# Fetching the tiles of v as pairs from one queue, in a decoder trunk with expert retrieval

## The chip, the cores and the metric

One core of one Trainium2 chip runs the whole program. The metric is device time in microseconds (us), the median of several executions. A profile of one execution shows where the time goes.

## What is computed

Two decoder layers over 256 positions of width 1024. Layer 0 mixes with attention and retention, layer 1 with a short gated convolution. Behind each mixer stands a product-key expert retrieval ("peer"): every token has 8 heads, each picks 16 of 16384 experts, and the output is the gated sum of their rows of v.

```python
def peer(xn, w_q, sub_keys, u, v):
    ...
    s1, i1 = lax.top_k(sc[:, :, 0], PEER_TOPK)
    s2, i2 = lax.top_k(sc[:, :, 1], PEER_TOPK)
    ...
    gate = jax.nn.softmax(top_s, axis=-1).astype(xn.dtype)
    ...
        hid = jax.nn.gelu(jnp.einsum('td,thkd->thk', tc, u[ec]), approximate=False)
        return jnp.einsum('thk,thkd->td', gc * hid, v[ec])
```

`u` and `v` are 16384 x 1024 in float32 for each layer, 64 MiB each.

## The kernel before

A layer's retrieval is done in two ways at once. For 160 tokens (`TD`) it is dense: all 128 tiles of u (128 experts x 1024, 512 KB) are multiplied with the tokens, the gates are put in where an expert was picked, and all 128 tiles of v are multiplied with the result. For the other 96 tokens (`TG`) rows of u and v are gathered: `Gather` issues indirect DMAs from POOL, each of 128 rows of 4 KB, 192 a layer, and DVE multiplies what has landed (line 1041 adds a row of v times its weight to `gacc`). `ga.step()` is called once a tile with a rate that spreads the rest of the gather over the tiles that are left; six tiles (`rows`, `grow`) hold rows.

The dense part has two stretches, here called u and v. In the v stretch tile i is used by PE for eight blocks of the output. Most tiles (those in `SPL`) are split first: ACT copies the raw tile into `vhi` in a shorter format (`weight_parts`, line 1419), DVE subtracts it from the raw tile into `vlo` (`weight_rest`, line 1426), and PE multiplies both (lines 1546 and 1548). A raw tile isn't read again after that subtraction. The tiles 0, 2, 12, 22, ... 122 and the last three are not split, PE reads them raw (line 1506). `carry(i)` does ACT's copy of tile i + 3 and DVE's subtraction of tile i + 2; then comes `st.next()` for tile i, then its matmuls. `vhi` and `vlo` have three buffers each.

All weights come through one ring, `Stream.ring`, with eight slots of 512 KB (`RAW`). `srcs` lists what is fetched and in which order. An entry of double width is fetched by one DMA into two neighbouring slots, as 8 KB a partition: the tiles of u are such pairs. The tiles of v are single, 4 KB a partition, and those with an odd number are issued by ACT (`src[2]`), all others by SP. `room()` says whether the next fetch may be written into the program: `free(i)` holds for a whole tile (its second entry is None) once `nu`, the count of tiles handed out, is past it. Engines run their own programs in order, and a DMA on a queue waits there for the last readers of its slot; so the place of a fetch in the program matters on ACT, among its copies, and little on SP, which does nothing else in these loops.

Of the kernel before, what the change touches and what calls it, by code (L numbers as in the profile page):

```python
# [19 lines left out]
P = 128  # L20
S = 256
D = 1024
# [6 lines left out]
NK = 128  # L29
# [8 lines left out]
STEPS = TG  # L38
SUB = 32
RAW = 8  # L40
# [9 lines left out]
for i in SPL:  # L50
    a, n = list(RUNS.items())[-1] if RUNS else (-9, 0)
# [69 lines left out]
class Stream:  # L121
# [6 lines left out]
    def __init__(self, ctx, tc, srcs):  # L128
        self.nc = tc.nc
        self.srcs = srcs  # L130
        pool = ctx.enter_context(tc.tile_pool(name="wraw", bufs=1))
        self.ring = pool.tile([P, RAW, D], F32, tag="raw", name="raw")
        self.hi_pool = ctx.enter_context(tc.tile_pool(name="whi", bufs=3))
        self.lo_pool = ctx.enter_context(tc.tile_pool(name="wlo", bufs=3))
        self.more = None
        self.end = 0
        self.raw = {}
        self.part = {}
        self.nl = 0
        self.held = 0  # L140
        self.ns = 0
        self.nu = 0

# [11 lines left out]
    def room(self):  # L155

        if self.nl >= len(self.srcs):
            return False
        n = 2 if self.srcs[self.nl][0].shape[-1] > D else 1
        return self.free(self.nl + n - 1 - RAW)  # L160

    def whole(self, i):
        return self.srcs[i][1] is None
# [23 lines left out]

    def free(self, i):

        return i < 0 or (i < self.nu - self.held if self.whole(i) else i < self.ns)  # L190

    def ahead(self, extra=0):
        n = len(self.srcs)
# [27 lines left out]


@with_exitstack
def trunk_kernel(ctx, tc, x, small, cst, mcst, ew_in, ew_out, ow_in, ow_out, wq, keys, pu, pe_, pv, pun, gains, out):
    nc = tc.nc
    v = nc.vector
    act = nc.scalar
# [15 lines left out]
    def peer_srcs(l):  # L243
        r = [(wq[l, f], f not in (1, 2)) for f in range(NPAIR)]
        for i in range(len(REST) // 2):
            r += [(pu[l, i], None), (None, None)]
        r += [(pv[l, i], None, i % 2 == 1) for i in range(NK)]
        return r

    srcs += peer_srcs(0)  # L250
    OF = [b * ND + k for k in range(ND) for b in (1, 2, 0)]
    srcs += [(ow_in[f], i > 1 and i % 2 == 1) for i, f in enumerate(OF)]
    srcs += [(ow_out[c], c % 2 == 0 and c < 6) for c in range(ND)]
    srcs += peer_srcs(1)

    h = pers.tile([P, 2, D], F32, tag="h", name="h")
# [10 lines left out]
    st = Stream(ctx, tc, srcs)  # L267
# [12 lines left out]
    def nm(s):  # L280
        uid[0] += 1
        return f"{s}{uid[0]}"
# [700 lines left out]
    class Gather:  # L983
# [29 lines left out]
        def issue(self):  # L1013

            while (self.open and self.i < self.TOTAL and (self.i < self.known or self.known == STEPS)
                   and self.i < self.c + len(self.rows)):
                s_ = self.i
                self.i += 1
                table = pun if s_ < STEPS else pv.rearrange("l i p d -> (l i p) d")
                gp.indirect_dma_start(self.row(s_), None, table,  # L1020
                                      bass.IndirectOffsetOnAxis(IG[:, 0, s_ % STEPS:s_ % STEPS + 1].bitcast(U32), 0))

# [30 lines left out]
    def peer(l, before, norm):  # L1053
        with tc.tile_pool(name=nm("hg"), bufs=1) as hp:
# [360 lines left out]
            def weight_parts(j, low=True):  # L1415

                raw = st.raw[first + j]
                whi[j] = st.hi_pool.tile([P, D], F32R, tag="hi", name=nm("vhi"))
                act.copy(whi[j], raw)  # L1419
                if low:  # L1420
                    weight_rest(j)

            def weight_rest(j):
                raw = st.raw[first + j]
                wlo[j] = st.lo_pool.tile([P, D], BF16, tag="lo", name=nm("vlo"))
                v.tensor_tensor(wlo[j], raw, whi[j].bitcast(F32), OP.subtract)  # L1426

            first = st.nu + NK - len(PRE)
            for i in range(NK):
# [82 lines left out]
            def carry(i):  # L1512
                j = i + AHEAD
                if "rest" in hsb:
                    row_rest()
                if 4 <= j and j in SPL:
                    if j in RUNS:
                        row_parts(j)
                    weight_parts(j, False)
                if 4 <= j - 1 and j - 1 in SPL:  # L1520
                    weight_rest(j - 1)
# [61 lines left out]
    with tc.manual_schedule():  # L1583
        norms = [Norm(0)]
        nc.sync.dma_start(G, small)
        nc.sync.dma_start(C[:, :P], cst[:, :P])
        for th in range(2):
            (nc.scalar if th else nc.sync).dma_start(h[:, th, :], x[th])
        nc.sync.dma_start(C[:, P:], cst[:, P:])
        v.memset(Z, 0.0)  # L1590
        act.activation(norms[0].w[:, 0, 6:7], Z[:, 0:1], AF.Sqrt)
        for _ in range(3):
            st._load()
        busy(24)
        norms[0].first(hid_tile(nm("junk")))
        a = Norm(1)
        even_mixer(norms[0], a)
        b = Folded(2)
        peer(0, a, b)
        a = Norm(3)  # L1600
        odd_mixer(b, a)
        peer(1, a, Final())
# [40 lines left out]
```

## Time and profile before

| What | Value |
|---|---|
| median of 3 runs | 1489.08 us (1485.73 to 1489.53) |
| the profiled execution, its own time | 1486.53 us |
| its span in the trace | 1484.7 us, granted clock 0.996 |
| busy share of PE, PEld, DVE, ACT, POOL | 97%, 89%, 84%, 54%, 49% |
| moved by DMA | 531.81 MB, mean 358 GB/s |
| fetches of v | 128 from SP, 128 from ACT, 512 KB each |
| fetches of u | 104 pairs from SP, 1024 KB each |
| indirect DMAs of rows | 192 of u, 192 of v |

PE is TensorE's matmuls, PEld its loading of weights, DVE VectorE, ACT ScalarE, POOL GpSimd, SP SyncE; a name with q is the queue of an engine. In a row "a<-b" the first name is written and the second read; "raw<-pv" is a fetch of a tile of v into the ring, "rows<-pv,ig" a gather of rows. The DMA share is the mean busy time of 16 DMA engines; since packets overlap a little at their ends, a full engine shows slightly over 1. The chain is the work that ended last, followed back from the end of the program.

### The profile page before, as it was taken

The page shows a single profiled execution, that of the slowest core. Times are in us where ns is not written, and L with a number is a line of the kernel's source. Part 1 is how long each engine was busy: PE and PEld are TensorE (multiplying, and loading weights), DVE is VectorE, ACT ScalarE, POOL GpSimd, SP SyncE. Part 2 cuts the span into 40 slices and gives each one's busy share as a digit, 9 for nine tenths or more (in the row PEclk, how much of TensorE's full clock was granted, in tenths as well). Part 3 has the DMA queues.
Part 4 walks back from the last instruction along what each step waited for, and adds up shares of the span by engine and source line. Part 5 has one row for each costly group of instructions (what it writes and reads, how often), then busy time and mean ns, then how long its engine had stood idle before and what let it go on. Part 6 is the DMA issues. An engine that isn't in the chain of part 4 may idle for free.

```text
span 1484.7 us, 30109 instructions
## 1 busy us (share of the span) xinstructions
PE 1434.1 (97%) x11260; PEld 1327.8 (89%) x11260; DVE 1242.5 (84%) x2505; ACT 804.1 (54%) x1872; POOL 731.1 (49%) x508
## 2 busy tenths in 40 slices
PE   9999999999998999899999999999999999999997
PEld 5667999999998999898898699999999999988887
DVE  5637999968898789999976589997888868999997
ACT  6556412158775555555663463213887745655554
POOL 6754545546664344443244374555655624653540
PEclk9999999999999999999999999999999999999999
DMA  8547899999999999999975589999999999999994
GB/s 323 198 146 253 324 369 393 397 413 412 411 412 407 385 398 405 402 407 408 384 264 180 179 307 346 388 402 404 411 413 410 402 392 396 389 407 406 405 408 172
DMA packets 132164, 531.81 MB, mean 358 GB/s; under 512 B 15217, under 2 KB 15473, under 8 KB 118705
## 3 DMA queue, kind: packets, MB, share of 16 engines
q1 hardware_dynamic: 57024, 257.95, 45.0%
q0 software_dynamic: 56416, 204.29, 34.8%
q10 hardware_dynamic: 18576, 67.64, 11.6%
q8 instruction: 89, 1.46, 0.4%
q14 instruction: 59, 0.48, 0.1%
HBM read 527.93 MB, written 1.05 MB: 356 GB/s over the span
## 4 chain that ended last, share of the span: by engine, by line
DMA 37%; PE 29%; DVE 24%; issue 5%; ACT 2%; POOL 1%; ACTq 0%; SPq 0%; DVEq 0%; POOLq 0%
DMA raw<-pv 25%; DMA rows<-pun,ig 7%; PE hid L1408 7%; DVE rows L1030 4%; PE vo L1546 4%; DMA grow<-pv,ig 3%; PE hid L291 2%; PE vo L1506 2%; DVE hg L1140 2%; DVE grow L1030 2%; DVE hg L1146 2%; DVE hg L1142 2%; PE vo L1548 2%; PE ea L325 2%; DMA rows<-pv,ig 2%
## 5 line engine op out<-in xcount | busy, mean ns | idle before, releaser
L1408 PE MATMUL hid<-xf,raw 128*128 128x160 f32 x3328 | 478.2, 301 | 8.8 <-DVE hg L1449 8.5
L1408 PEld LDWEIGHTS hid<-xf,raw 128*128 128x128 f32 x3328 | 458.2, 191 | 11.7 <-DVE hg L1449 11.6
L1419 ACT CAST vhi<-raw 128x1024 fp32r<-128x1024 f32 x222 | 227.4, 1047 | 205.7 <-DMA raw<-pv 143.1
L1546 PE MATMUL vo<-ko,vhi 128*128 128x320 f32 x1776 | 315.2, 319 | 14.8 <-DVE ko L1496 9.6
L1426 DVE TENSOR_TENSOR vlo<-raw,vhi 128x1024 bf16<-128x1024 f32 x222 | 268.0, 1223 | 47.6 <-ACT vhi L1419 43.2
L1020 POOL DMA_INDIRECT rows<-pv,ig x128 | 199.8, 1561 | 216.4 <-DVE gacc L1041 172.0
L1546 PEld LDWEIGHTS vo<-ko,vhi 128*128 128x128 f32 x1776 | 262.0, 188 | 21.3 <-ACT vhi L1419 14.2
L1020 POOL DMA_INDIRECT rows<-pun,ig x128 | 161.3, 1260 | 118.6 <-DVE rows L1030 61.6
L176 POOL TENSOR_TENSOR lo<-raw,hi 128x1024 bf16<-128x1024 f32 x70 | 167.2, 2397 | 87.0 <-ACT hi L174 80.3
L1030 DVE SCALAR_TENSOR_TENSOR rows<-rows,xg 128x1024 f32<-128x1024 f32 x128 | 155.4, 1220 | 23.6 <-DMA rows<-pun,ig 23.1
L1548 PE MATMUL vo<-hb,vlo 128*128 128x160 bf16 x1776 | 161.4, 234 | 7.1 <-DVE vlo L1426 6.8
L1446 ACT ACTIVATE hg<-hid 128x160 f32<-128x160 f32 (+14 forms) x240 | 62.2, 265 | 194.1 <-PE hid L1408 193.9
L1041 DVE SCALAR_TENSOR_TENSOR gacc<-rows,ghid,gacc 128x1024 f32<-128x1024 f32 x124 | 158.8, 1281 | 6.5 <-DMA rows<-pv,ig 6.2
L1020 POOL DMA_INDIRECT grow<-pv,ig x64 | 91.8, 1434 | 117.9 <-DVE gacc L1041 103.1
L1548 PEld LDWEIGHTS <-vlo 128*128 128x128 bf16 x1776 | 117.4, 98 | 34.1 <-DVE vlo L1426 14.3
L1358 ACT ACTIVATE ko<-ko,idxT 128x128 f16<-128x128 f16 x320 | 101.6, 391 | 38.2 <-DVE ko L1343 38.1
L1020 POOL DMA_INDIRECT grow<-pun,ig x64 | 82.8, 1293 | 78.9 <-DVE grow L1030 50.2
L174 ACT CAST hi<-raw 128x1024 fp32r<-128x1024 f32 x100 | 102.4, 1046 | 30.2 <-issue 19.9
L291 PE MATMUL hid<-x,hi 128*128 128x256 f32 x800 | 108.9, 289 | 3.9 <-DVE z L973 2.0
L291 PEld LDWEIGHTS hid<-x,hi 128*128 128x128 f32 x800 | 100.0, 193 | 4.8 <-issue 2.9
L1361 ACT ACTIVATE ko<-ko,idxT 128x128 f16<-128x128 f16 x320 | 101.2, 389 | 0.0
L1506 PE MATMUL vo<-hg,raw 128*128 128x160 f32 x544 | 83.1, 302 | 1.1 <-DVE hg L1449 1.1
(254 smaller groups left out, 2075.6 us busy)
## 6 DMA issues: line engine op xcount, KB each, us to landing
raw<-pu SPq DMA_DIRECT2D x104, 1024.0 KB, 8.3
raw<-pv SPq DMA_DIRECT2D x128, 512.0 KB, 8.5
raw<-pv ACTq DMA_DIRECT2D x128, 512.0 KB, 7.9
raw<-wq SPq DMA_DIRECT2D x32, 512.0 KB, 4.2
raw<-ew_in SPq DMA_DIRECT2D x28, 512.0 KB, 4.4
raw<-ow_in SPq DMA_DIRECT2D x24, 512.0 KB, 4.9
hg<-pe_ SPq DMA_DIRECT2D x22, 512.0 KB, 6.9
raw<-ew_out SPq DMA_DIRECT2D x8, 512.0 KB, 3.3
```

The source lines that it names most:

```text
L174: self.nc.scalar.copy(hi, t)
L176: eng.tensor_tensor(lo, t, hi.bitcast(F32), OP.subtract)
L291: pe.matmul(ps[:, :S], hi[:, k * P:(k + 1) * P], A2[:, k, s_, :], start=k == 0 and s_ == 0, stop=False)
L1020: gp.indirect_dma_start(self.row(s_), None, table, bass.IndirectOffsetOnAxis(IG[:, 0, s_ % STEPS:s_ % STEPS + 1].bitcast(U32), 0))
L1030: v.scalar_tensor_tensor(r, r, 1.0, XG[:, q % 2, :], op0=OP.mult, op1=OP.mult, accum_out=w)
L1041: v.scalar_tensor_tensor(self.acc[q], r, w, self.acc[q], op0=OP.mult, op1=OP.add)
L1408: pe.matmul(ps[:, :TD], w[k], XF[:, k, :], start=k == 0, stop=k == ND - 1)
L1419: act.copy(whi[j], raw)
L1426: v.tensor_tensor(wlo[j], raw, whi[j].bitcast(F32), OP.subtract)
L1506: pe.matmul(vo[b][:, TG:S], w[:, c], HG[:, i, :], stop=i == NK - 1, **m)
L1546: pe.matmul(vo[b][:, TG:S + TD], hi[:, b * P:(b + 1) * P], hs, **m)
L1548: pe.matmul(vo[b][:, TG:S], lo[:, b * P:(b + 1) * P], hb, **m)
```

## The change

The tiles of v are listed as pairs like those of u, so that one DMA from SP brings two tiles. ACT issues none. A pair needs both slots free. `dead` is a set of ring entries whose raw tile has been told to be split to the end: `weight_rest` puts a tile in and at once lets the stream write the fetches that this makes possible. Since the array of v is laid out for pairs now, the gather reads from a second copy of v in plain order, `pvn`.

```diff
+        self.dead = set()
...
         n = 2 if self.srcs[self.nl][0].shape[-1] > D else 1
-        return self.free(self.nl + n - 1 - RAW)
+        return all(self.free(self.nl + j - RAW) for j in range(n))
...
-        return i < 0 or (i < self.nu - self.held if self.whole(i) else i < self.ns)
+        return i < 0 or i in self.dead or (i < self.nu - self.held if self.whole(i) else i < self.ns)
...
-        r += [(pv[l, i], None, i % 2 == 1) for i in range(NK)]
+        for i in range(NK // 2):
+            r += [(pv[l, i], None), (None, None)]
...
-                table = pun if s_ < STEPS else pv.rearrange("l i p d -> (l i p) d")
+                table = pun if s_ < STEPS else pvn
...
                 v.tensor_tensor(wlo[j], raw, whi[j].bitcast(F32), OP.subtract)
+                st.dead.add(first + j)
+                st.loads()
...
-        "pv": ct(a["peer_v"].reshape(2, NK, P, D)),
+        "pv": ct(a["peer_v"].reshape(2, NK // 2, 2, P, D).transpose(0, 1, 3, 2, 4)).reshape(2, -1, P, 2 * D),
+        "pvn": ct(a["peer_v"].reshape(2 * NK * P, D)),
```

The order of instructions on PE and DVE stays as it was. On ACT, in the v stretch of layer 0, the rows around the copy of tile 23 were these (`vhi_5219`; the fetch behind it is that of tile 27, and the one behind `vhi_5266` that of tile 29):

```order
L1488 CAST ko_4767<-hg_1210 128x3x160
L1489 CAST hb_5216<-hg_1210 128x480 [waits PE_49]
L1419 CAST vhi_5219<-raw 128x1024 [waits DMAHW3_49,DVE_49,PE_49]
L151 DMA raw<-pv 128x1024
L1419 CAST vhi_5243<-raw 128x1024 [waits DMAHW1_49,DVE_49,PE_49]
L1419 CAST vhi_5266<-raw 128x1024 [waits DMAHW5_49,DVE_49,PE_49]
L151 DMA raw<-pv 128x1024 [waits DMAHW7_49]
```

And now (`vhi_5207` is the copy of tile 23):

```order
L1492 CAST ko_4763<-hg_1210 128x3x160
L1493 CAST hb_5204<-hg_1210 128x480 [waits PE_49]
L1421 CAST vhi_5207<-raw 128x1024 [waits DMAHW5_49,DVE_49,PE_49]
L1421 CAST vhi_5230<-raw 128x1024 [waits DMAHW6_49,DVE_49,PE_49]
L1421 CAST vhi_5252<-raw 128x1024 [waits DVE_49,PE_49]
```

The fetches are gone from ACT, and its copies follow each other.

On SP, before, the rows are the fetches of the tiles 12, 14, 16, 18, 20 and 22. The one of tile 20 waits for PE, since its slot held tile 12, which isn't split:

```order
L151 DMA raw<-pv 128x1024 [waits DMAHW6_49,DMAHW5_49,DVE_49]
L151 DMA raw<-pv 128x1024 [waits DMAHW0_49,DVE_49]
L151 DMA raw<-pv 128x1024 [waits DMAHW2_49,DVE_49]
L151 DMA raw<-pv 128x1024 [waits DMAHW4_49,DMAHW3_49,DVE_49]
L151 DMA raw<-pv 128x1024 [waits DMAHW5_49,PE_49]
L151 DMA raw<-pv 128x1024 [waits DMAHW7_49,DMAHW6_49,DVE_49]
```

And now, the pairs from (12, 13) to (22, 23):

```order
L152 DMA raw<-pv 128x2048 [waits DMAHW4_49,DVE_49]
L152 DMA raw<-pv 128x2048 [waits DMAHW5_49,DVE_49]
L152 DMA raw<-pv 128x2048 [waits DMAHW6_49,DVE_49]
L152 DMA raw<-pv 128x2048 [waits DMAHW7_49,DVE_49]
L152 DMA raw<-pv 128x2048 [waits DMAHW0_49,DVE_49,PE_49]
L152 DMA raw<-pv 128x2048 [waits DMAHW1_49,DVE_49]
```

There are as many rows as before, each twice as wide. The pair (20, 21) waits for DVE and for PE, and what stands behind it waits with it.

More of the change, by code (lines that the diff above doesn't have):

```diff
@@ L223, in trunk_kernel @@
 @with_exitstack
-def trunk_kernel(ctx, tc, x, small, cst, mcst, ew_in, ew_out, ow_in, ow_out, wq, keys, pu, pe_, pv, pun, gains, out):
+def trunk_kernel(ctx, tc, x, small, cst, mcst, ew_in, ew_out, ow_in, ow_out, wq, keys, pu, pe_, pv, pvn, pun, gains, out):
     nc = tc.nc
```

## The prediction

> **What bounds the kernel now.** I read the page first (busy shares, slices, chain), then the windows, then the DMA queues of two windows, then the chain in order of time.
>
> ```profile
> span 1484.7 us, 30109 instructions
> PE 1434.1 (97%) x11260; PEld 1327.8 (89%) x11260; DVE 1242.5 (84%) x2505; ACT 804.1 (54%) x1872; POOL 731.1 (49%) x508
> ...
> DMA  8547899999999999999975589999999999999994
> ...
> DMA raw<-pv 25%; DMA rows<-pun,ig 7%; PE hid L1408 7%; DVE rows L1030 4%; PE vo L1546 4%; DMA grow<-pv,ig 3%; PE hid L291 2%; PE vo L1506 2%; DVE hg L1140 2%; DVE grow L1030 2%; DVE hg L1146 2%; DVE hg L1142 2%; PE vo L1548 2%; PE ea L325 2%; DMA rows<-pv,ig 2%
> ...
> raw<-pu SPq DMA_DIRECT2D x104, 1024.0 KB, 8.3
> raw<-pv SPq DMA_DIRECT2D x128, 512.0 KB, 8.5
> raw<-pv ACTq DMA_DIRECT2D x128, 512.0 KB, 7.9
> ```
>
> PE's 97% is modelled and hides waits, so it decides nothing. The chain puts 25% of the span, 371 us, on fetches of tiles of v: 256 fetches of 512 KB (134.2 MB), half from SP, half from ACT. That is exactly what the change touches. The windows say whether those waits are latency or bandwidth (columns: busy time of PE, PEld, DVE, ACT, POOL, then clock, DMA share, GB/s):
>
> ```profile
> 335.00:370.00 35.00, 35.00 (x298) 34.66 (x298) 29.64 (x67) 29.88 (x114) 22.03 (x18) 1.00 1.02 413
> 482.00:510.00 28.00, 27.08 (x219) 26.02 (x219) 18.89 (x23) 15.53 (x25) 6.35 (x4) 1.00 0.99 384
> 510.00:546.00 36.00, 36.00 (x319) 34.57 (x319) 31.79 (x31) 20.12 (x25) 18.06 (x11) 1.00 1.01 398
> 580.00:620.00 40.00, 36.84 (x306) 33.24 (x307) 36.25 (x34) 22.78 (x30) 14.68 (x10) 1.00 1.02 407
> 660.00:700.00 40.00, 37.28 (x317) 34.22 (x314) 36.51 (x35) 23.99 (x30) 14.88 (x11) 1.00 1.02 408
> 1300.00:1340.00 40.00, 36.74 (x303) 32.65 (x302) 36.59 (x35) 24.00 (x30) 21.69 (x11) 1.00 1.02 404
> ```
>
> In the v stretch the DMA engines are full (1.02) and move 404 to 408 GB/s; in the u stretch, with the same share, 413. So v is bound by what a byte costs on the DMA engines, except at its start, where PE sets the pace. The chain (start, length, what) gives the bounds of the stretch, 482 to about 738 us in layer 0 and 1204 to about 1455 in layer 1, and its two kinds of links:
>
> ```profile
> 482.37 8.75 DMA raw<-pv
> ...
> 508.92 1.21 PE vo L1546 x8
> 510.13 0.57 PE vo L1548 x8
> ...
> 565.52 7.79 DMA raw<-pv
> ...
> 573.41 0.02 ACT vhi L1419
> 573.43 9.09 DMA raw<-pv
> ...
> 732.65 1.28 DVE gacc L1041
> 737.62 2.21 PE vo L1506 x16
> ...
> 1203.91 8.05 DMA raw<-pv
> ...
> 1455.24 1.29 DVE gacc L1041
> ```
>
> First PE works tile behind tile, 1.78 us each. Later each link is one landing of about 8 us, a cast that starts on it, and at once the next fetch from ACT. At some 2.0 us a tile a link spans 4 tiles: a fetch from ACT goes out when the tile 4 ahead of its own has landed.
>
> **What a byte costs.** Queue q1 is SP's, q10 ACT's, q0 the rows of the gather (columns: packets, MB, share of 16 engines). First 300 to 460 us (u, fetched as pairs), then 580 to 700 us (v, single tiles):
>
> ```profile
> DMA packets 14197, 66.01 MB, mean 413 GB/s; under 512 B 1563, under 2 KB 1563, under 8 KB 10738
> q0 software_dynamic: 10322, 37.59, 58.7%
> q1 hardware_dynamic: 3857, 28.19, 42.8%
> ```
>
> ```profile
> DMA packets 13341, 48.69 MB, mean 406 GB/s; under 512 B 1481, under 2 KB 1481, under 8 KB 13329
> q0 software_dynamic: 4827, 17.58, 36.7%
> q1 hardware_dynamic: 4314, 15.71, 33.0%
> q10 hardware_dynamic: 4188, 15.24, 32.1%
> ```
>
> Share times window times 16 over MB gives engine time per MB. Pairs of u (8 KB a partition): 0.428 x 160 x 16 / 28.19 = 38.9 us. Single tiles of v (4 KB): 0.330 x 120 x 16 / 15.71 = 40.3 from SP, 0.321 x 1920 / 15.24 = 40.4 from ACT. The gather, 4 KB rows in both, is the control: 0.587 x 2560 / 37.59 = 40.0 and 0.367 x 1920 / 17.58 = 40.1. So it isn't the stretch that makes v dearer, it is the short rows: 1.5 us per MB, 3.8%.
>
> **The change part by part.**
>
> Single tiles become pairs. If every byte of v were on the path: 134.2 MB x 1.5 / 16 = 12.6 us less. On the path are 371 us of the 507 us of both v stretches, 73%: 9.2 us. By the rates alone (406 to 413 GB/s, 1.7% of 371 us) it is 6.3 us. I take 9, the queues' own figure, since the control supports it, and keep 6.3 and 12.6 as ends.
>
> The start of v. Here PE is the bound and cheaper bytes bring nothing by themselves; they can only fill the ring further before the engines become the bound. One more tile in the ring is worth its fetch, 0.524 MB at 406 GB/s, 1.3 us, once a layer; none is worth 0, two in each layer 5 us. There is room for it: the DMA share falls to 0.99 there, and the gather pauses (waits from 470 to 500 us: total, times, longest):
>
> ```profile
> POOL rows L1020 <- DVE gacc L1041: 13.9, 1, 13.9
> ```
>
> I take 1 us for both layers together. Steady work minus 9, start minus 1: minus 10.
>
> ACT issues 128 fetches less, SP as many as before but of double size (durations in ns of the issues, then waits, from 580 to 720 us).
>
> ```profile
> L151 ACTq DMA_DIRECT2D raw<-pv x34: 333/334/335, 582.6 to 717.6; - x34
> ACT vhi L1419 <- DMA raw<-pv: 48.7, 28, 2.6
> SPq L151 <- DVE vlo L1426: 91.8, 25, 6.4
> SPq L151 <- PE vo L1506: 35.5, 7, 7.0
> ```
>
> 128 x 0.334 us = 43 us of ACT's queue is taken away and I cost it at 0: it runs beside the cast that precedes it (573.41 and 573.43 above), and ACT waits 48.7 of the 140 us from 580 for landings anyway. Were that cover gone, it would be a gain, of 43 us at most.
>
> When a pair may start. Tile k+8 from SP waits for the subtraction of tile k; tile k+4 from ACT for the landing of tile k. Afterwards the pair waits for the subtractions of both tiles it replaces, and everything behind it on SP with it. The first tile of a pair so goes out about one tile later than it did, 2 us; the second, which went out 4 tiles ahead of use, now goes out some 6 ahead. Bounds: each start 2 us late and uncovered at the 24 unsplit tiles from 12 to 122 would cost 48 us; the looser second tile could gain up to what DVE leaves (below). Between them I take 0, because the row it is nearest to is the DMA share of 1.02: work is always queued on the engines, so a later start lengthens a queue and costs no time. If that cover is gone, the third rival decides.
>
> The set of dead slots moves fetches earlier in the program only. In the v loop SP issues nothing but these fetches, and each still waits for its slot's readers: 0. Nothing else stands behind them on SP there.
>
> The table of rows has the same 4 KB rows, bytes and issues on POOL: 0. POOL is idle half of the span (49% busy above), and no queue is moved past it.
>
> Sum: the profiled execution took 1486.53 us, 1.8 us around its span, so 1476.5. The median of the runs is 1489.08, 2.6 above the profiled one, which gives 1479.
>
> **What is late next.** DVE, not PE (546 to 721 us):
>
> ```profile
> 546.00:721.00 175.00, 163.87 (x154) 1.00 1.02 405
> L1426 DVE TENSOR_TENSOR vlo<-raw,vhi 128x1024 bf16<-128x1024 f32 x78 | 93.9, 1223 | 11.0 <-ACT vhi L1419 8.6 <-PE vo L1506 1.5 <-PE vo L1546 0.5
> ```
>
> It is busy 163.87 of 175 us, 93.6%; a stretch shorter by 2.5% leaves it at 96%. No gain beyond 6.4% of 371 us, 24 us, is possible there.
>
> **The rivals.**
>
> Nothing to see. The rows' length doesn't matter, and the 406 of v is the mix. For it: when nothing but single 4 KB tiles is fetched (750 to 800 us, 40 slices), slices reach 413 too.
>
> ```profile
> GB/s 0 56 354 410 367 413 397 410 397 161 305 102 144 347 320 385 387 413 397 318 197 82 347 177 295 269 138 0 184 292 285 236 243 33 285 161 341 52 0 0
> ```
>
> Against it: the gather's own rows cost the same in u and v. Then only the start of v gains, 1 us: 1488, with 1485 to 1492 around it. A rule speaks for this rival: the Trainium skill, "DMA: Bandwidth & Descriptors", Specifications, puts the smallest transfer for line rate at 512 B, by which rows of 4 KB are as good as 8 KB and the steady term would be 0 instead of 9 us. The queue rows above, 40.4 against 38.9, disagree with it.
>
> The ring was the bound. The links of 4 tiles set the pace, and the full engines are only what that leaves; then issuing further ahead frees v up to DVE's limit. Against it: a share of 1.02 with nothing to spare. At most 24 us: 1465.
>
> Pairs starve the engines. Every tenth tile (12, 22, ...) isn't split, its slot is free only when PE has done with it (the 7 waits of 35.5 us above), and now its neighbour and all later pairs wait with it; the tile before a pair's second can't be used until both have landed. For it: SP already waits 5.1 us each time. Against it: three pairs and several rows are queued meanwhile. Price: d us at each of the 24 unsplit tiles; it decides from 0.4 us on, where 24 d eats the 10 us. At 1 us, half a tile's time: 1479 + 24 = 1503.
>
> **How the numbers follow.** About 0.3%, 4.5 us, is what a measurement of this kernel tells from no change: below 1484.6 is faster, above 1493.5 slower. Cheaper bytes, 1472 to 1484: 0.52. The ring, 1463 to 1472: 0.12. Nothing to see, 1485 to 1492: 0.21. Starved engines, 1494 and up: 0.15. Faster 0.64, same 0.21, slower 0.15. The likeliest is 1479. The range from 1465 to 1491 holds the first, nearly all of the second and most of the third.
>
> **What would show it.** Right: in the v stretch the fetches cost about 39 us per MB on q1, the rate is 412 to 415 GB/s at a share of 1.02, the chain's share on fetches of v falls by some 9 us, DVE is busier than 95%, and u and the mixers keep their lengths. The ring as the bound: a v stretch more than 8 us shorter in each layer with the cost per MB unchanged. Nothing to see: q1 at 40 and 406 GB/s. Starved: the DMA share below 1.0 in steady v, and casts that wait longer after each unsplit tile. The prediction fails above all if the engines run dry between pairs, or if DVE and PE, each above 90%, cannot close up as far as the DMA allows.

## The result and the profile after

The changed kernel took 1478.76 us in the median of 7 runs (1473.74 to 1481.83), the kernel before 1486.33 beside it: ratio 0.9931, interval 0.9912 to 0.9949, faster by some 10 us (8 to 13 by the interval). The forecast was 1479, from a median before of 1489.08 (a ratio of 0.9932). The profiled execution took 1473.74 us, span 1472.0; it is the fastest of the seven, so its span is 12.7 us below the one before, where the means of the runs differ by 9.3.

The page, the lines that answer to those of before:

```profile
span 1472.0 us, 29967 instructions
PE 1428.2 (97%) x11260; PEld 1327.3 (90%) x11260; DVE 1238.5 (84%) x2505; ACT 805.0 (55%) x1872; POOL 775.8 (53%) x508
...
PE 48%; DVE 26%; DMA 18%; issue 5%; ACT 2%; POOL 1%; DVEq 0%; SPq 0%; POOLq 0%; ACTq 0%
PE hid L1410 14%; PE vo L1550 10%; DMA rows<-pvn,ig 7%; DMA grow<-pvn,ig 6%; PE vo L1552 5%; DVE rows L1032 3%; PE vo L1510 3%; DMA rows<-pun,ig 2%; PE hid L293 2%; DVE gacc L1043 2%; DVE vlo L1428 2%; DVE hg L1142 2%; DVE grow L1032 2%; DVE hg L1148 2%; DVE hg L1144 2%
...
raw<-pv SPq DMA_DIRECT2D x128, 1024.0 KB, 9.3
```

Fetches of v held 25% of the chain; now they aren't in this list. PE's products of v (`vo`) and gathered rows of v (`rows<-pvn`, `grow<-pvn`, 13% together) stand there. Where the time came from shows in PE's order of time: the first products of a split tile of v in layer 0, the first of layer 1's mixer, the first products of a split tile of v in layer 1, before and after:

```profile
494.05 1.44 PE L1546 MATMUL vo<-ko,vhi 128*128 128x320 f32 x8
751.43 2.18 PE L308 MATMUL hid<-x,hi 128*128 128x256 f32 x16
1214.90 1.44 PE L1546 MATMUL vo<-ko,vhi 128*128 128x320 f32 x8
```

```profile
493.93 1.45 PE L1550 MATMUL vo<-ko,vhi 128*128 128x320 f32 x8
745.02 2.18 PE L310 MATMUL hid<-x,hi 128*128 128x256 f32 x16
1206.64 1.44 PE L1550 MATMUL vo<-ko,vhi 128*128 128x320 f32 x8
```

v of layer 0 took 257.4 us and takes 251.1; from there to v of layer 1 463.5 and 461.6; from there to the end of the span 269.8 and 265.4. So 10.7 of the 12.7 us of span come out of the two v stretches (the last one with the end of the program behind it). In the windows and queues of the changed kernel (columns as before the change; queues from 580 to 700 us):

```profile
482.00:510.00 28.00, 27.25 (x221) 26.19 (x220) 18.91 (x23) 15.62 (x25) 6.47 (x4) 1.00 1.02 410
510.00:546.00 36.00, 36.00 (x319) 34.57 (x317) 31.69 (x31) 20.12 (x25) 18.82 (x11) 1.00 0.99 391
580.00:620.00 40.00, 39.81 (x350) 37.47 (x349) 39.97 (x40) 25.00 (x32) 22.91 (x12) 1.00 1.02 415
660.00:700.00 40.00, 38.11 (x327) 35.28 (x326) 38.94 (x37) 24.36 (x31) 26.97 (x12) 1.00 1.02 415
```

```profile
DMA packets 9207, 49.77 MB, mean 415 GB/s; under 512 B 1017, under 2 KB 1017, under 8 KB 5262
q1 hardware_dynamic: 4418, 32.21, 65.1%
q0 software_dynamic: 4776, 17.39, 36.1%
...
raw<-pv SPq DMA_DIRECT2D x30, 1024.0 KB, 9.7
rows<-pvn,ig POOLq DMA_INDIRECT x24, 18.2
grow<-pvn,ig POOLq DMA_INDIRECT x11, 19.4
```

0.651 x 1920 / 32.21 is 38.8 engine us per MB for the fetches, where 40.4 stood; the gather stays at 0.361 x 1920 / 17.39 = 39.9. The engines are as full as before and move 415 GB/s, not 406. PE (39.81 of 40 us) and DVE (39.97) still set the pace at 580 to 620 us, where the kernel before already waited for fetches. The new thing is in the last two rows: gathered rows land after 18 to 19 us, where they took 11. The chain from 600 us on goes over them:

```profile
605.20 1.36 PE vo L1550 x8
...
617.45 19.90 DMA grow<-pvn,ig
...
671.94 17.94 DMA rows<-pvn,ig
689.98 1.30 DVE gacc L1043
691.53 20.16 DMA rows<-pvn,ig
```

DVE's waits from 470 to 735 us say the same. First the kernel before, then the changed one (total us, times, longest):

```profile
DVE vlo L1426 <- ACT vhi L1419: 21.0, 25, 3.3
```

```profile
DVE vlo L1428 <- ACT vhi L1421: 12.0, 8, 3.2
DVE gacc L1043 <- DMA rows<-pvn,ig: 6.4, 5, 2.2
DVE gacc L1043 <- DMA grow<-pvn,ig: 1.4, 2, 1.2
```

### The profile page after: what moved, and what is told of

Same layout as the page of the kernel before. It is cut to its first block, busy times and chain, and to the rows that moved or that the text cites. A ratio compares the mean times of both kernels' runs of the same rounds, so it can differ in the third digit from the quotient of the medians.

```text
span 1472.0 us, 29967 instructions
## 1 busy us (share of the span) xinstructions
PE 1428.2 (97%) x11260; PEld 1327.3 (90%) x11260; DVE 1238.5 (84%) x2505; ACT 805.0 (55%) x1872; POOL 775.8 (53%) x508
## 4 chain that ended last, share of the span: by engine, by line
PE 48%; DVE 26%; DMA 18%; issue 5%; ACT 2%; POOL 1%; DVEq 0%; SPq 0%; POOLq 0%; ACTq 0%
PE hid L1410 14%; PE vo L1550 10%; DMA rows<-pvn,ig 7%; DMA grow<-pvn,ig 6%; PE vo L1552 5%; DVE rows L1032 3%; PE vo L1510 3%; DMA rows<-pun,ig 2%; PE hid L293 2%; DVE gacc L1043 2%; DVE vlo L1428 2%; DVE hg L1142 2%; DVE grow L1032 2%; DVE hg L1148 2%; DVE hg L1144 2%
## 5 line engine op out<-in xcount | busy, mean ns | idle before, releaser
L1022 POOL DMA_INDIRECT rows<-pvn,ig x128 | 226.1, 1767 | 185.3 <-DVE gacc L1043 144.1
L1022 POOL DMA_INDIRECT grow<-pvn,ig x64 | 111.6, 1743 | 95.0 <-DVE gacc L1043 76.1
L1043 DVE SCALAR_TENSOR_TENSOR gacc<-grow,ghid,gacc 128x1024 f32<-128x1024 f32 x62 | 79.3, 1279 | 9.3 <-DMA grow<-pvn,ig 9.1
```

What stands on the lines that cost most here:

```text
L1022: gp.indirect_dma_start(self.row(s_), None, table, bass.IndirectOffsetOnAxis(IG[:, 0, s_ % STEPS:s_ % STEPS + 1].bitcast(U32), 0))
L1043: v.scalar_tensor_tensor(self.acc[q], r, w, self.acc[q], op0=OP.mult, op1=OP.add)
```

## Taking the change apart

The total came out as forecast, but a total can be right by terms that cancel. The theory is that rows of 8 KB are cheaper than rows of 4 KB. The rivals are that fetches go out further ahead, that there are fewer DMAs, that the dead slots or the second table matter. Four kernels ran on one chip to hold these apart, beside the kernel before; the changed kernel itself did not run there.

**Single tiles, all from SP.**

```diff
-        for i in range(NK // 2):
-            r += [(pv[l, i], None), (None, None)]
+        r += [(pv[l, i], None) for i in range(NK)]
```

> The changed kernel, but the tiles of v are fetched singly again (512 KB, 4 KB a partition), all of them by SP, with the dead slots and the second table kept. Theory 'short rows cost more': the queue of SP costs 40.0 to 40.6 engine us per MB in the v stretch, 404 to 408 GB/s, and the time is that of the kernel before, ratio 0.998 to 1.001. Rival 'issuing further ahead' (ACT's fetches only 4 tiles ahead were the bound): the cost per MB stays at 40 and the gain is there all the same, ratio 0.991 to 0.995.

Ratio 0.9979 (0.9964 to 0.9994), 3.1 us below the kernel before, just outside what the first theory allowed and a third of what the rival wanted. This kernel differs from the one before in two ways, since odd tiles may go out further ahead and ACT is rid of its fetches; no run holds the two apart.

**Pairs by one DMA, but two rows of 4 KB a partition.**

```diff
-            r += [(pv[l, i], None), (None, None)]
+            r += [(pv[l, 2 * i:2 * i + 2].rearrange("n p d -> p n d"), None), (None, None)]
...
-        "pv": ct(a["peer_v"].reshape(2, NK // 2, 2, P, D).transpose(0, 1, 3, 2, 4)).reshape(2, -1, P, 2 * D),
+        "pv": ct(a["peer_v"].reshape(2, NK, P, D)),
```

> The changed kernel, one DMA from SP for two tiles as there, but from the plain array, so that each partition takes two rows of 4 KB from two places and not one of 8 KB. Theory 'short rows cost more': 40 engine us per MB on SP's queue, about 406 GB/s, ratio 0.998 to 1.002. Rival 'fewer DMAs' (half the DMAs, half the completion writes): about 39 per MB and ratio 0.991 to 0.995 as in the changed kernel. Rival 'issuing further ahead': 40 per MB, ratio 0.991 to 0.995.

Ratio 1.0022 (1.0008 to 1.0036), 3.3 us slower than before: just above what the first theory allowed, and far from both rivals. The queues from 580 to 700 us of the two kernels, single tiles first:

```profile
q1 hardware_dynamic: 8494, 30.93, 64.6%
...
raw<-pv SPq DMA_DIRECT2D x60, 512.0 KB, 13.3
rows<-pvn,ig POOLq DMA_INDIRECT x23, 9.0
```

```profile
q1 hardware_dynamic: 8031, 30.96, 64.5%
...
raw<-pv SPq DMA_DIRECT2D x30, 1024.0 KB, 11.5
rows<-pvn,ig POOLq DMA_INDIRECT x22, 8.8
```

0.646 x 1920 / 30.93 = 40.1 and 0.645 x 1920 / 30.96 = 40.0 engine us per MB: half the DMAs cost the engines the same. The changed kernel differs from this one in the length of the rows alone, and there the fetches cost 38.8 and 415 GB/s are moved, not 408. What lowers the cost is the length of the rows.

**The dead slots taken away.**

```diff
-                st.dead.add(first + j)
-                st.loads()
```

> The changed kernel without the two lines that put a tile into the set of dead slots and write the fetches at once; a slot is told free when its tile is handed to PE, as before. Theory 'place on SP doesn't matter': the fetches wait for the same readers, ratio 0.992 to 0.995 and 415 GB/s in the v stretch. Rival 'told earlier is issued earlier': a pair goes out up to two tiles (4 us) later, casts wait longer, ratio 0.997 or more.

Ratio 0.9934 (0.9914 to 0.9955), 415 GB/s from 580 to 700 us, as in the changed kernel: the place of a fetch in SP's program is worth nothing that these runs, good to some 2 us, can show.

**The table alone, in the kernel before.**

```diff
-                table = pun if s_ < STEPS else pv.rearrange("l i p d -> (l i p) d")
+                table = pun if s_ < STEPS else pvn
```

> The kernel before with only the second copy of v for the gather added (the fetches stay single, from SP and ACT). Theory 'same rows, same bytes': ratio 0.999 to 1.001, the gather at 40 engine us per MB. Rival 'the gather and the fetches got in each other's way in one array': ratio 0.997 or less and a gather that lands sooner than 11 us.

Ratio 1.0006 (0.9991 to 1.0021): nothing beyond 2 us either way.

Side by side on that chip, means and their differences with some 95%: moving all single fetches to SP is worth minus 3.1 us. Pairing them there with short rows costs 7.2 (5.0 to 9.5) on top. Lengthening the rows to 8 KB, seen against the kernel without dead slots, gains 13.3 (10.8 to 15.8). The three make minus 9.2, what that last kernel shows (0.9934) and about what the change shows (0.9931).

The last two steps hang together, since a row of 8 KB can't be had here without a pair. From single tiles on SP to pairs of long rows it is minus 6.1 us (3.8 to 8.3); the plus 7.2 and the minus 13.3 hold for the way over pairs of short rows. The price per MB explains some 10 of the 13.3: (40.0 - 38.8) x 134.2 / 16 = 10.1 us if every byte of v counts. So long rows probably also took away a part of what pairing costs with short ones.

Where the 7.2 us of pairing go isn't settled by a run of its own. The start of v shows part of it. These are the first 26 us of v in layer 0 and in layer 1, counted from its first product, for single tiles, for pairs of short rows and for the changed kernel:

```profile
490.00:516.00 26.00, 23.31 (x186) 22.05 (x184) 18.78 (x20) 15.86 (x22) 7.84 (x4) 0.93 0.93 356
1210.00:1236.00 26.00, 25.28 (x215) 24.01 (x215) 22.53 (x23) 17.89 (x25) 8.36 (x6) 1.00 0.98 374
```

```profile
490.00:516.00 26.00, 22.92 (x182) 21.45 (x181) 18.83 (x22) 15.43 (x22) 7.25 (x4) 0.93 0.89 334
1214.00:1240.00 26.00, 22.78 (x182) 21.51 (x181) 18.96 (x20) 15.47 (x22) 5.57 (x4) 0.93 0.85 326
```

```profile
490.00:516.00 26.00, 25.25 (x215) 23.99 (x214) 21.44 (x23) 17.87 (x25) 10.23 (x5) 1.00 1.00 393
1204.00:1230.00 26.00, 25.89 (x219) 24.59 (x217) 23.22 (x24) 17.65 (x25) 9.16 (x6) 1.00 0.97 382
```

With short pairs the engines' share falls to 0.89 and 0.85, and in layer 1 PE works 2.5 us less than with single tiles. The changed kernel has 1.00 and 0.97: its pairs of long rows show no such hole. In steady v singles and short pairs both stand at 408 GB/s and a share of 1.02 to 1.03.

## What bounds it now

**Every second pair from ACT.**

```diff
-            r += [(pv[l, i], None), (None, None)]
+            r += [(pv[l, i], None, i % 2 == 1), (None, None)]
```

> The changed kernel, but every second pair of v is issued by ACT, so that two queues carry pairs beside the gather's. Theory 'turns by queue': rows of 8 KB from two queues against rows of 4 KB from one leave the gather less, its rows land later than 18 us and DVE waits longer for them, ratio 0.995 to 1.000. Rival 'one queue or two is the same once the engines are full': 415 GB/s, 39 engine us per MB, gather as in the changed kernel, ratio 0.991 to 0.995.

Ratio 0.9939 (0.9918 to 0.9961). The rows of the gather land after 16.2 us, not later than 18, so the first theory fell: a second queue of pairs takes nothing more from the gather, and one queue or two makes no difference to the time that these runs show. The changed kernel did not run beside it.

**A ring of six slots.**

```diff
-RAW = 8
+RAW = 6
```

> The changed kernel with a ring of six slots instead of eight, in all stretches. It sizes what the ring is worth. Theory 'engines are kept full by enough fetches in flight': with three pairs the share falls below 1.0 in the v stretch, casts wait longer, ratio 1.005 to 1.03, while the gather lands sooner than 18 us. Rival 'the ring doesn't matter as long as bytes bind': ratio 0.992 to 0.998.

Ratio 1.0222 (1.0195 to 1.0249), 33 us slower than the kernel before. The ring is smaller in all stretches, but most of the loss lies in v: in layer 0, from the first product of v to the first of the mixer, 275.2 us (496.48 to 771.72) where the changed kernel takes 254.2 (490.85 to 745.02). In steady v, and in the queues from 580 to 700 us:

```profile
580.00:620.00 40.00, 35.72 (x296) 32.51 (x296) 34.86 (x33) 22.00 (x28) 22.01 (x11) 1.00 1.00 390
...
q1 hardware_dynamic: 4051, 29.52, 62.6%
q0 software_dynamic: 4641, 16.89, 35.8%
...
rows<-pvn,ig POOLq DMA_INDIRECT x22, 10.6
```

390 GB/s instead of 415, and gathered rows land after 10.6 us again. The share falls little, to 1.00 here and 0.98 to 0.99 from 620 to 700 us. The rest of the loss stands in the price: 0.626 x 1920 / 29.52 = 40.7 engine us per MB for the fetches and 0.358 x 1920 / 16.89 = 40.7 for the gather, though both rows kept their lengths. Why isn't shown. So a ring of six costs time in steady v; whether single tiles would suffer as much from it wasn't run.

**Half the bytes of v.** Only the first tile of each pair is fetched; the second slot keeps old data, all other work stays.

```diff
+        if n == 2 and self.pvs and self.pvs[0] == i:
+            self.pvs.pop(0)
+            eng.dma_start(self.ring[:, s_, :], src[0][:, :D])
```

> The changed kernel with only the first tile of each pair of v fetched (the second slot keeps what was there, so the output is not that of the reference): half the bytes of v, all other work as it was. Theory 'v is bound by bytes, DVE is next': each v stretch falls to what DVE needs, 1.87 us a tile or some 236 us, the share falls below 0.8, ratio 0.972 to 0.985. Rival 'already bound by DVE and PE after the change': no more than 4 us below the changed kernel, ratio 0.990 or more.

Ratio 0.9795 (0.9768 to 0.9823), about 20 us below the changed kernel's ratio. From its windows and its chain:

```profile
580.00:620.00 40.00, 39.81 (x351) 37.52 (x350) 39.96 (x38) 27.26 (x34) 30.29 (x12) 1.00 0.89 303
...
PE 57%; DVE 24%; DMA 13%; issue 4%; ACT 1%; POOL 1%; DVEq 0%; SPq 0%; POOLq 0%; ACTq 0%
```

This is the floor of the other engines, PE and DVE full side by side: v of layer 0 takes 243.3 us (493.09 to 736.42), not the 236 expected. After the change, 8 us of v in layer 0 still hang on what the DMA engines have to move.

**A seventh tile for rows.** In the v stretch the tokens' tile `XF` is idle and can hold gathered rows.

```diff
+        def one_more(self):
+            self.rows.append(XF.rearrange("p k t -> p (k t)")[:, :D])
+            self.spare.append(self.rows[-1])
+            self.issue()
...
             ga.rate = (ga.TOTAL - ga.c) / (NK - 6.5)
+            ga.one_more()
```

> The changed kernel with a seventh tile for gathered rows in the v stretch (the tile that held the tokens for u is free there); before it were six. Theory 'bytes still bind' (415 GB/s at a share of 1.02): only the start of v, where the gather pauses with all its tiles full, can gain, 0.524 MB or 1.3 us in each layer: ratio 0.991 to 0.994, 0 to 3 us below the changed kernel. Rival 'the gather is the new wait' (its rows land after 18 us where they took 11, and the chain runs over them): a seventh tile gives 3.3 us more time to land, DVE's waits for rows go, ratio 0.987 to 0.990.

Ratio 0.9895 (0.9876 to 0.9915). That lies in the rival's range, and the interval reaches into the other theory's; since the changed kernel did not run beside it, both ran again on one chip:

> The changed kernel itself, as the mark for the two kernels that run beside it: ratio 0.991 to 0.995.

> Seven tiles for gathered rows in the v stretch, now on the same chip as the changed kernel. Theory 'bytes still bind': 0 to 3 us below it, so a ratio 0.000 to 0.002 lower than its own. Rival 'the gather is the new wait': 0.003 or more lower.

The changed kernel: 1476.41 us, ratio 0.9929 (0.9908 to 0.9949). With seven tiles: 1472.49 us, 0.9908 (0.9889 to 0.9927); the means differ by 3.4 us (1.5 to 5.3). It is the fastest kernel of this study that fetches all of v. Two rows of each window view show where the two differ, the changed kernel of that chip first:

```profile
510.00:546.00 36.00, 36.00 (x319) 34.47 (x318) 31.71 (x31) 20.13 (x26) 18.82 (x11) 1.00 1.01 391
620.00:660.00 40.00, 37.99 (x333) 35.76 (x332) 35.89 (x35) 24.61 (x31) 22.29 (x12) 1.00 1.02 415
```

```profile
510.00:546.00 36.00, 36.00 (x317) 34.47 (x315) 31.70 (x31) 20.02 (x25) 18.82 (x11) 1.00 1.01 406
620.00:660.00 40.00, 39.63 (x349) 37.52 (x348) 38.58 (x37) 25.80 (x34) 27.08 (x13) 1.00 1.02 415
```

More is moved at the start of v, 406 against 391 GB/s, and PE and DVE are busier from 620 to 660 us; in steady v the rate is the same 415. By this view the theory of bytes looks right, but 3.4 us lies between its 0 to 3 and the rival's 0.003 (4.5 us), and the interval covers both. DVE's waits for gathered rows fall too, though the rows land even later (20.8 us): from 10.1 to 8.7 us in layer 0 and from 9.4 to 6.8 in layer 1, 4 us in all, as much as the gain.

Two kernels stepped the gather from the first tile of v on, with `if i > 1:` taken off `ga.step()`:

> Seven tiles for rows, and the gather is stepped from the first tile of v on, not from the third. Theory 'bytes still bind': what is left to gain is the start of v, where the share is 0.99 to 1.01; 0 to 2 us below the kernel with seven tiles. Rival 'PE sets the pace there': no difference from it, within 1 us, or a loss, since DVE's work on rows delays the first subtractions.

> The changed kernel with the gather stepped from the first tile of v on. Theory 'bytes still bind': two rows are asked for some 4 us sooner in each layer, 0 to 2 us below the changed kernel. Rival as for the run before: no difference or a loss of 1 us.

1473.0 us (0.9909) with seven tiles, 1476.02 us (0.9933) with six: no difference from the kernels beside them, 0.5 us each with 2 us of uncertainty, as their rival said. The kernel with six tiles moves more at the start without gaining by it:

```profile
510.00:546.00 36.00, 36.00 (x318) 34.56 (x315) 31.14 (x31) 20.04 (x26) 17.91 (x10) 1.00 1.02 412
```

412 GB/s against 391, at the same time. So the bytes moved at the start of v don't explain what the seventh tile gains, and its cause stays open.

## The prediction, point by point

**Right: what bounds the kernel.** v was bound by what a byte costs on the DMA engines. The cost fell to 38.8 us per MB and the rate rose to 415 GB/s at the same share, both as named beforehand. The sign on the chain was too small: its share on fetches of v was to fall by some 9 of 371 us, and it went over to PE, DVE and gathered rows almost altogether. DVE is at 167 of 175 us from 546 to 721, 95.5% where more than 95% was said:

```profile
546.00:721.00 175.00, 169.09 (x1469) 158.34 (x1468) 167.19 (x158) 109.83 (x138) 102.14 (x51) 1.00 1.01 412
```

**Uncertain in size: the steady term.** Taken were 9 us, because 73% of v was on the chain, with 12.6 as the upper end. Long rows in place of short ones, both in pairs, measured 13.3 (10.8 to 15.8), of which the prices explain 10.1 with all of v counted; pairs of long rows in place of single tiles on SP measured 6.1. The cut to 73% looks wrong: in layer 0 PE sets the pace longer now, since the first transfer on the chain behind the start of v stands at 617 us where it stood at 547, so bytes saved while PE sets the pace can stay in the ring. But of these 70 us 45 come with single tiles from SP already (592), whose rows are as short as before; with short pairs it stands at 580.

**Not 0 with short rows: "when a pair may start".** With short rows pairing costs 7.2 us. The reason given for 0, a share of 1.02, holds in steady v but not at the start of that kernel (0.89 and 0.85). In the changed kernel (1.00 and 0.97) the trace shows no such loss, and how much of the 7.2 it still pays isn't shown. The prediction's bounds, up to 48 us of loss, did contain it. Unsplit tiles as its place, the third rival, aren't seen: SP waits for them 2.5 us from 580 to 720 us, where it waited 35.5.

```profile
SPq L152 <- PE vo L1510: 2.5, 3, 1.1
```

**Missing: fetches from SP alone.** The prediction had 1 us for a fuller ring at the start, and 0 for ACT's issues and for odd tiles that go out further ahead than 4. Moving single fetches from ACT to SP is worth 3.1 us (0.9 to 5.3) by itself; which of the two brings it isn't shown. The second rival, that the ring was the bound, can hold for that much and no more.

**Right as far as the runs can tell: dead slots and table at 0.** 0.9934 without the dead slots, 1.0006 for the table alone; half the pairs back on ACT give 0.9939. Each is good to some 2 us.

**Too low: the limit of 24 us.** Half the bytes gave 30 us (0.9795). The limit was taken from DVE's idle time from 546 to 721 us and from the 73% alone; where the other 6 us lie is open.

So minus 10 was the sum of minus 9, minus 1 and 0. What the runs fix is minus 3 for singles on SP and minus 6 from there to pairs of long rows; over pairs of short rows the latter is plus 7 and minus 13. The mechanism, cheaper bytes by longer rows, is shown. That the total came out to the microsecond is luck: it left out the 3 us of fetches from SP and what pairing costs, and these work against each other.

**Not asked at all: who gets the engines.** The prediction didn't say that gathered rows would land after 18 us where they took 11. With short rows in the one queue they land after 9, with long ones after 18, while fetches go from 13.3 or 11.5 to 9.7. Engines that take turns between queues row by row would do that, since rows of double length take about double time. But it isn't the whole account. Beside the pairs of u, which have rows of 8 KB as well, gathered rows land after 10.5 us (kernel before, 300 to 460 us), beside pairs of v in a ring of six after 10.6, beside pairs on two queues after 16.2:

```profile
rows<-pun,ig POOLq DMA_INDIRECT x34, 10.5
```

So the length of the rows isn't all that decides, and no run settles the rule. The Trainium skill, "DMA: Bandwidth & Descriptors", Queues, rings and completion order, says that an engine goes round the queues it has work for packet by packet, and drains a whole packet of one queue before it switches. The 9 and 18 us beside one queue agree with that, the 16.2 us beside two show no further loss for the gather.

## What to carry to other kernels

Where full DMA engines bound a stretch, compare the engine time per MB of each queue between stretches, with a queue whose rows keep their length as a control; that price times the bytes is an estimate of the gain, and work saved while another engine sets the pace may count as long as a buffer can hold it. Cost the granularity of a larger transfer apart from its price per byte, at the start of the stretch above all, since the two may have opposite signs; and where one can't be had without the other, don't take the steps of one order for terms that simply add. After a change of row length, look at what other queues on the same engines now wait.

## What the runs showed of the hardware

On full engines (a share of 1.01 to 1.03, from 580 to 700 us) rows of 8 KB a partition cost 38.7 to 38.9 engine us per MB, rows of 4 KB 39.8 to 40.4 (the gather's included), whether fetched by one DMA for two tiles or by two, and from SP or from ACT. That is 3 to 4% of the bytes' time; pairs of long rows ran 13.3 us faster than pairs of short ones. With a ring of six (0.98 to 1.00) both lengths cost 40.7, so the price is to be compared at the same load only. The Trainium skill, "DMA: Bandwidth & Descriptors", Specifications, puts line rate at 512 B and more; the trace agrees that 4 KB is near it but not that nothing is left above.
